# A hybrid S5 and gated DeltaNet trunk on one core: values of the memory by tokens, early inputs of layer 1's output projection, the memory's norm at fixed places

## The chip, the core and the metric

The kernel runs on one core of a Trainium2 chip. A core has five engines with queues of their own, which work in order: TensorE (PE in the profile; it multiplies, and its weight loads are shown as PEld), VectorE (DVE), ScalarE (ACT), GpSimd (POOL) and SyncE (SP, which here only issues DMA transfers). The metric is the device time of one execution in microseconds, lower is better; the median of several runs counts.

## The reference

Two layers run over 1024 tokens of width 1024. Layer 1 has an S5 mixer, layer 2 a gated DeltaNet mixer; each layer also attends to 256 tokens of a memory with 4 heads. Cut to what the change touches:

```python
h = rmsnorm(x, norm_w[i])
mem_h = rmsnorm(mem, mem_norm_w[i])            # 256 x 1024
...                                            # the mixer: y_mix, 1024 x 1536
kv = mem_h @ w_kv[i]                           # 256 x 1024: 512 of keys, 512 of values
y_x = cross_attn(q_x, k, v) * silu(gate_x)     # 1024 x 512
x = x + concatenate([y_mix, y_x]) @ w_out[i]   # 1024 x 2048 by 2048 x 1024
...
return rmsnorm(x, final_norm_w)
```

In the S5 layer, `y_mix` is `y * sigmoid(y @ w_glu + b_glu)` times a gate.

## The kernel before

All large products run in three parts: each operand is split into a rounded high part and a rest (`split`, line 86 the cast by ACT, line 73 the subtraction by DVE), and `mm3` (line 48) issues high x high, high x low, low x high. A weight tile (`weight`) is loaded to `wraw` (512 KB for 128 x 1024), cast to `whi` by ACT, and its rest `wlo` is made by DVE or, with "both", half by DVE and half by POOL. `project` multiplies such tiles with a stack of inputs into PSUM buffers named `pp`, of which there are four; everything small uses four others, `ps_a`.

A scheduler orders each engine's instructions by priority, except where `self.pe.on` keeps TensorE in the order of the code. Tiles come from pools, and a new tile waits until the one that had its memory is done with.

**The head.** `memory_inputs` loads the memory, transposed, as `memT` (4 transfers of 256 KB). `memory(0)` splits it into `mh` and `ml`, weighted by the norm's weights, and then makes eight tiles of `kv`, channels on partitions: each is 24 products over 256 memory tokens. A tile is multiplied by `mrow`, the norm's factor of each token laid along a row, into `kvt`. Tiles 0 to 3 are keys and are stored. Tiles 4 to 7 are values, which the attention wants by tokens: two transposes on TensorE (line 51, `ps_a<-ident,kvt`) and a copy by ACT (`kvu`) follow. The norm itself is `memory_norm`: squares (`msq`), sums (`macc`), the root (`mnv`, `mne`, ...), and two products that spread it (`mndg`).

Beside it run the eight tiles of x: ACT makes `hh`, DVE `hl`, ACT or POOL the square `sq`, DVE adds it to `acc`. Then come two tiles of the S5 input product, `memory(1)` for the second layer, DVE's chain of S5 parameters, and two more tiles.

**The output projection of layer 1.** The twelve gated columns (`w_glu`, inputs `yh` and `yl`) end with a sigmoid and a product on DVE, and each is stored to DRAM as `yT[ct]`. The attention has stored its results as `yT[12]` to `yT[15]`. The 16 inputs of the first half of the tokens are loaded back as `yr` (256 KB each; eight buffers, so eight are loaded ahead) and split into `oh` and `ol`; these tiles lie where tiles of the gate lay, and wait until those are done with. TensorE takes them in the order 12, 13, 14, 15, 0, ..., 11. A second half of the tokens follows.

**The tail.** The last column is done in two blocks of 256 tokens. While the first block is scaled (`out_scale`), DVE works on the norm of the second (`fzv`, `fze`, `fzt`, `fndg`). `beside` names the tiles that ACT and POOL scale instead of DVE.

## Time and profile before

| | |
|---|---|
| median of 3 runs | 1933.11 us (1930.89 to 1936.47) |
| profiled execution, its own time | 1939.14 us |
| its span in the trace | 1937.4 us |
| mean granted clock of TensorE | 0.984 |
| TensorE's first product | 10.98 us after the span's start |
| busy: PE, DVE, ACT, POOL | 96%, 66%, 49%, 5% of the span |

The profiled execution is 6.0 us slower than the median. In rows of the timeline the first two columns are the start, in us from the span's start, and the length; a bracket at the end is the time in which the engine was idle before it, and what ended that. Rows of stretches give the stretch, its length, the engine's busy time with the count of instructions, the granted clock, the DMA engines' share and GB/s.

### The profile page before, as it was taken

The page shows a single profiled execution, that of the slowest core. Times are in us where ns is not written, and L with a number is a line of the kernel's source. Part 1 is how long each engine was busy: PE and PEld are TensorE (multiplying, and loading weights), DVE is VectorE, ACT ScalarE, POOL GpSimd, SP SyncE. Part 2 cuts the span into 40 slices and gives each one's busy share as a digit, 9 for nine tenths or more (in the row PEclk, how much of TensorE's full clock was granted, in tenths as well). Part 3 has the DMA queues.
Part 4 walks back from the last instruction along what each step waited for, and adds up shares of the span by engine and source line. Part 5 has one row for each costly group of instructions (what it writes and reads, how often), then busy time and mean ns, then how long its engine had stood idle before and what let it go on. Part 6 is the DMA issues. An engine that isn't in the chain of part 4 may idle for free.

```text
span 1937.4 us, 28738 instructions
## 1 busy us (share of the span) xinstructions
PE 1865.1 (96%) x10390; PEld 1533.5 (79%) x10390; DVE 1284.0 (66%) x2508; ACT 958.1 (49%) x2043; POOL 95.8 (5%) x65
## 2 busy tenths in 40 slices
PE   6899999999989998999999999999999999899997
PEld 6788888788878887788778878877777888688886
DVE  7988898896565412564455555988743776789744
ACT  5345688786455421543343456665343653544421
POOL 3000000000201221000000000000000000000000
PEclk9999999999999999999999999999999999999999
DMA  7445655655854353654312467676445764876752
GB/s 229 151 136 136 165 170 157 168 155 146 254 167 133 116 173 102 210 164 141 120 56 97 132 199 235 218 224 198 132 117 197 226 202 146 265 231 197 201 161 87
DMA packets 258942, 325.17 MB, mean 168 GB/s; under 512 B 80753, under 2 KB 182705, under 8 KB 258801
## 3 DMA queue, kind: packets, MB, share of 16 engines
q1 hardware_dynamic: 233456, 238.40, 39.9%
q10 hardware_dynamic: 25344, 84.95, 14.7%
q8 instruction: 82, 1.34, 0.3%
q14 instruction: 60, 0.48, 0.1%
HBM read 213.20 MB, written 93.95 MB: 159 GB/s over the span
## 4 chain that ended last, share of the span: by engine, by line
PE 80%; DVE 7%; DMA 6%; ACT 4%; issue 2%; SPq 1%; DVEq 0%; ACTq 0%
PE pp L48 64%; PE ps_a L48 13%; PE ps_a L51 3%; DMA zr<-oTd 1%; SPq L70 1%; DVE wlo L73 1%; DMA yr<-gy 1%; ACT whi L86 0%; DVE pr L77 0%; DMA E<-Grow 0%; DVE ol L73 0%; ACT pr L330 0%; DMA XM<-Dm 0%; DMA R<-E 0%; DMA wraw<-in_s_w_in_dram 0%
## 5 line engine op out<-in xcount | busy, mean ns | idle before, releaser
L48 PE MATMUL pp<-hh,whi 128*128 128x512 f32 x1216 | 496.0, 408 | 0.0
L48 PE MATMUL pp<-hl,whi 128*128 128x512 f32 x1216 | 478.9, 394 | 2.8 <-DVE hl L82 2.8
L48 PE MATMUL pp<-hh,wlo 128*128 128x512 f32 x1216 | 478.0, 393 | 0.0
L86 ACT CAST whi<-wraw 128x1024 fp32r<-128x1024 f32 (+1 forms) x180 | 183.7, 1022 | 370.6 <-PE pp L48 347.0
L73 DVE TENSOR_TENSOR wlo<-wraw,whi 128x1024 fp32r<-128x1024 f32 (+2 forms) x180 | 212.9, 1183 | 94.4 <-ACT whi L86 93.2
L48 PEld LDWEIGHTS pp<-hh,whi 128*128 128x128 f32 x1216 | 229.7, 189 | 50.8 <-issue 5.3
L48 PEld LDWEIGHTS pp<-hh,wlo 128*128 128x128 f32 x1216 | 229.3, 189 | 48.9
L48 PEld LDWEIGHTS pp<-hl,whi 128*128 128x128 f32 x1216 | 230.1, 189 | 46.0 <-DVE hl L82 3.8
L48 PE MATMUL pp<-oh,whi 128*128 128x512 f32 (+1 forms) x528 | 207.8, 394 | 5.7 <-ACT oh L86 5.5
L48 PE MATMUL pp<-oh,wlo 128*128 128x512 f32 (+1 forms) x528 | 210.0, 398 | 0.1
L48 PE MATMUL pp<-ol,whi 128*128 128x512 f32 (+1 forms) x528 | 208.4, 395 | 1.3 <-DVE ol L73 1.3
L48 PEld LDWEIGHTS pp<-oh,whi 128*128 128x128 f32 x528 | 100.9, 191 | 29.0 <-ACT oh L86 7.7
L48 PEld LDWEIGHTS pp<-ol,whi 128*128 128x128 f32 x528 | 100.6, 191 | 25.8 <-DVE ol L73 3.5
L48 PEld LDWEIGHTS pp<-oh,wlo 128*128 128x128 f32 x528 | 101.0, 191 | 21.2 <-DVE wlo L73 0.8
L48 PE MATMUL pp<-yl,whi 128*128 128x512 f32 x288 | 114.2, 396 | 0.4 <-DVE yl L73 0.4
L48 PE MATMUL pp<-yh,wlo 128*128 128x512 f32 x288 | 114.2, 396 | 0.0
L48 PE MATMUL pp<-yh,whi 128*128 128x512 f32 x288 | 113.7, 395 | 0.0
L73 DVE TENSOR_TENSOR pj<-pp,hr 128x512 f32<-128x512 f32 x104 | 69.0, 686 | 54.8 <-PE pp L48 54.8
L73 DVE TENSOR_TENSOR cx<-pp,hr 128x512 f32<-128x512 f32 x48 | 32.5, 689 | 93.6 <-PE pp L48 93.6
L82 DVE SCALAR_TENSOR_TENSOR pj<-cx,conv_w,pj 128x1024 f32<-128x1024 f32 x72 | 92.4, 1283 | 1.4
L48 PEld LDWEIGHTS pp<-yl,whi 128*128 128x128 f32 x288 | 54.4, 189 | 12.4 <-DVE yl L73 0.8
L48 PEld LDWEIGHTS pp<-yh,wlo 128*128 128x128 f32 x288 | 54.4, 189 | 11.9
(363 smaller groups left out, 3109.2 us busy)
## 6 DMA issues: line engine op xcount, KB each, us to landing
wraw<-in_w_out_dram ACTq DMA_DIRECT2D x64, 512.0 KB, 4.1
wraw<-in_g_w_in_dram ACTq DMA_DIRECT2D x44, 512.0 KB, 3.9
wraw<-in_s_w_in_dram ACTq DMA_DIRECT2D x32, 512.0 KB, 4.0
R<-E SPq DMA_DIRECT2D x48, 256.0 KB, 3.9
gate<-pj SPq DMA_DIRECT2D x24, 512.0 KB, 4.4
qkv<-pj SPq DMA_DIRECT2D x24, 512.0 KB, 2.6
kq<-qkv SPq DMA_DIRECT2D x60, 192.0 KB, 4.3
wraw<-in_w_glu_dram ACTq DMA_DIRECT2D x24, 384.0 KB, 3.5
```

What stands on the lines that cost most here:

```text
L48: return self.pin(self.eng.matmul(*a, **kw))
L51: return self.pin(self.eng.transpose(*a, **kw))
L70: self.nc.sync.dma_start(out=out, in_=in_)
L73: (eng or self.v).tensor_tensor(out=out, in0=a, in1=b, op=op)
L82: self.v.scalar_tensor_tensor(out=out, in0=a, scalar=s, in1=b, op0=op0, op1=op1)
L86: self.act.copy(hi, src)
```

## The change

Three parts.

**A. The memory.** The values are computed by tokens: the memory's tokens are now the stationary operand, and two weight tiles side by side the moving one, so the result needs no transpose. There are as many products as before. ACT scales the result with the token's factor, a scalar per partition (`mcol`). The values come first, then the four keys, in the order of the code. The first two joined value weights are loaded among the pieces of `memT`. The two sums of the norm are adds instead of reductions, and its products stand behind the values (`macc`) and behind the third key (`mndg`).

On TensorE, at layer 0's values: before, a value tile's product stood beside the transposes of the tile before.

```order
L48 MATMUL pp<-ml,whi 128x256
L51 MATMUL ps_a<-ident_150,kvt 128x128 x2
L48 MATMUL pp<-mh,wlo 128x256
L51 MATMUL ps_a<-ident_150,kvt 128x128 x2
L48 MATMUL pp<-mh,whi 128x256
```

Now, at the end of the values, where the keys begin:

```order
L48 MATMUL pp<-whi,mh 128x256
L48 MATMUL pp<-wlo,mh 128x256
L48 MATMUL pp<-whi,ml 128x256
L48 MATMUL ps_a<-ones_155,macc_350 128x1 x2
L48 MATMUL pp<-mh,whi 128x256
L48 MATMUL pp<-ml,whi 128x256
```

The first value pair has two buffers of `ps_a`, the second two of `pp`. On ACT, at the first x tiles, it stood before (`kvu` is the copy behind the transposes):

```order
L86 CAST whi<-wraw 128x1024
L278 COPY kvu<-ps_a 128x256 x2
L179 ACTIVATE sq<-x 128x1024
L237 ACTIVATE hh_167<-x,nw_158 128x1024
L86 CAST whi<-wraw 128x1024
L278 COPY kvu<-ps_a 128x256
L86 CAST whi<-wraw 128x1024
```

and now (the cast ahead of the first `hh` waits for the second key's last product that reads the older weight; TensorE's first product of the third key waits for the `kvu<-pp` row):

```order
L86 CAST whi<-wraw 128x1024
L313 ACTIVATE kvu<-ps_a,mcol_381 128x2x128 x2
L86 CAST whi<-wraw 128x1024
L242 ACTIVATE hh_167<-x,nw_158 128x1024
L184 ACTIVATE sq<-x 128x1024
L242 ACTIVATE hh_167<-x,nw_158 128x1024
L184 ACTIVATE sq<-x 128x1024
L313 ACTIVATE kvu<-pp,mcol_381 128x2x128 x2
L242 ACTIVATE hh_167<-x,nw_158 128x1024 x2
```

The scalings moved behind two x tiles.

**B. The projection's inputs.** At gated column 10, five of the 16 inputs of the first half (12 to 15 and 0) are loaded and split into tiles of the attention's pool, which stays open. Ten of the other eleven are loaded straight into `oh` and `ol` tiles that are not yet used and cast in place; the last comes through `yr` (four buffers instead of eight). The stores of `yT[10]` and `yT[11]` are issued by POOL instead of SP. On SP, from the store of column 7 on, before:

```order
L70 DMA yT<-ye 128x1024
L70 DMA ge<-gate_92 128x1024
L70 DMA yT<-ye 128x1024 x3
L70 DMA abw_7022<-in_g_w_ab_dram 128x192
L70 DMA yT<-ye 128x1024
L70 DMA yr<-yT 128x512 x17
```

and now (the two last stores are on POOL):

```order
L70 DMA ge<-gate_92 128x1024
L824 DMA yT<-ye 128x1024 x2
L70 DMA abw_7006<-in_g_w_ab_dram 128x192
L70 DMA oh_7051<-yT 128x512
L70 DMA ol_7055<-yT 128x512
L70 DMA oh_7059<-yT 128x512
L70 DMA ol_7063<-yT 128x512
```

The loads moved ahead of the last stores.

On TensorE, the first row being the last gated product, before:

```order
L48 MATMUL pp<-yh_5230,wlo 128x512
L48 MATMUL pp<-oh_7035,whi 128x512
L48 MATMUL pp<-ol_7036,whi 128x512
L48 MATMUL pp<-oh_7035,wlo 128x512
L48 MATMUL pp<-oh_7037,whi 128x512
```

and now, with the early inputs first:

```order
L48 MATMUL pp<-yh_5190,wlo 128x512
L48 MATMUL pp<-qh,whi 128x512
L48 MATMUL pp<-ql,whi 128x512
L48 MATMUL pp<-qh,wlo 128x512
L48 MATMUL pp<-ph,whi 128x512
L48 MATMUL pp<-pl,whi 128x512
L48 MATMUL pp<-ph,wlo 128x512
L48 MATMUL pp<-ph,whi 128x512
```

Fifteen products on `qh` to `pr` stand where the first `oh` stood; the order of the gated columns and of the attention among them is as before.

**C. The tail.** For the first block of the last column, two more tiles (4 and 6) are scaled by ACT and POOL. On DVE, in the norm's chain of the second block, before:

```order
L77 TENSOR_SCALAR fzh<-fzv 128x2
L82 SCALAR_TENSOR_TENSOR xo_17426<-xo_17426,fnw_159,ps_a 128x256
L79 TENSOR_SCALAR fze<-fze 128x2
L82 SCALAR_TENSOR_TENSOR xo_17562<-xo_17562,fnw_159,ps_a 128x256
L82 SCALAR_TENSOR_TENSOR fzt<-fze,fzh 128x1 x2
```

and now:

```order
L77 TENSOR_SCALAR fzh<-fzv 128x2
L79 TENSOR_SCALAR fze<-fze 128x2
L82 SCALAR_TENSOR_TENSOR fzt<-fze,fzh 128x1 x2
L82 SCALAR_TENSOR_TENSOR fze<-fzt,fze 128x2
L82 SCALAR_TENSOR_TENSOR fzt<-fze,fzh 128x1 x2
```

The two long rows left the chain.

The diff (lines that the memory's old functions lose are left out; they stand above):

```diff
             self.dma(self.mnw, self.A["mnw"])
             self.act.copy(self.once(wp, (128, 1), "table"), self.ones[:, 0:1])
+            self.first = []
+            for q, step in ((0, 2), (1, 4)):
+                w = [self.ring.tile([128, 8, 128], dt, name=n, tag=n)
+                     for n, dt in (("wraw", F32), ("whi", F32R), ("wlo", F32R))]
+                self.first.append(w[1:])
+                for k in range(4 * q, 4 * q + 4, step):
+                    raw, hi, lo = (t.rearrange("p (c k) n -> p c k n", c=2)[:, :, k % 4:k % 4 + step] for t in w)
+                    self.dma(raw, self.A["w_kv"][0, 4:6, :, k:k + step].rearrange("c p k n -> p c k n"))
+                    for j in range(k, k + step, 2):
+                        self.dma(mt[:, j:j + 2], self.A["memT"][j:j + 2].rearrange("k p t -> p k t"))
+                    self.split(raw, hi, lo)
+    def memory_sum(self, wp):
         acc = self.once(wp, (128, 256), "macc")
         for k in range(0, 8, 4):
             sq = self.tl(wp, (128, 4, 256), "msq")
             self.act.activation(sq, self.memT[:, k:k + 4], AF.Square)
             part = acc if k == 0 else self.tl(wp, (128, 256), "kvt", bufs=2)
+            self.tt(sq[:, 0:2], sq[:, 0:2], sq[:, 2:4], ADD)
+            self.tt(part, sq[:, 0], sq[:, 1], ADD)
         self.tt(acc, acc, part, ADD)
+        col = self.negative_rstd(wp, (acc,), 1024, "mn")
+        self.mcol = self.once(wp, (128, 2), "mcol")
+        self.ts(self.mcol, col, -1.0, MUL)
+    def value_weight(self, layer, i, q):
+        ct = 4 + 2 * i
+        return self.weight(self.A["w_kv"][layer, ct:ct + 2, :, 4 * q:4 * q + 4, :].rearrange("c p k n -> p c k n"))
     def memory(self, layer, wp):
         mt = self.memT
         hh, hl = self.tl(wp, (128, 8, 256), "mh", F32R), self.tl(wp, (128, 8, 256), "ml", F32R)
         for k in range(8):
             self.weighted(mt[:, k], self.mnw[:, layer, k:k + 1], hh[:, k], hl[:, k])
+        pairs = []
+        for i in range(2):
+            pool, nm = ((self.pa, "ps_a"), (self.pp, "pp"))[i]
+            ps = [pool.tile([128, 256], F32, name=nm, tag=nm) for _ in range(2)]
+            for q in range(2):
+                w = self.first[q] if layer == i == 0 else self.value_weight(layer, i, q)
+                rows = [t.rearrange("p (c k) n -> p k c n", c=2) for t in w]
+                for j in range(4):
+                    k = 4 * q + j
+                    for b in range(2):
+                        s = slice(128 * b, 128 * b + 128)
+                        self.mm3(ps[b].rearrange("p (c n) -> p c n", c=2), (hh[:, k, s], hl[:, k, s]),
+                                 [t[:, j] for t in rows], k == 0, k == 7)
+            pairs.append(ps)
         if layer == 0:
+            self.memory_sum(wp)
+        def key(ct, ps):
             t = self.tl(wp, (128, 256), "kvt", bufs=2)
             self.tt(t, ps, self.mrow, MUL)
             self.dma(self.kvd[layer][ct], t)
+        def values(i, ps):
+            t = self.tl(wp, (128, 2, 2, 128), "kvu", bufs=1)
+            for b in range(2):
+                self.act.activation(t[:, :, b], ps[b].rearrange("p (c n) -> p c n", c=2), AF.Copy,
+                                    scale=self.mcol[:, b:b + 1])
+            for c in range(2):
+                self.dma(self.kvd[layer][4 + 2 * i + c], t[:, c].rearrange("p b d -> p (b d)"))
+        todo = []
+        for ct in range(4):
+            if ct == (0 if layer else 2):
+                for i, ps in enumerate(pairs):
+                    values(i, ps)
+            ps, = self.project([self.A["w_kv"][layer, ct]], (hh, hl), n=256)
+            todo.append((ct, ps))
+            if layer == 0 and ct == 2:
+                self.mrow = self.once(wp, (128, 256), "mrow")
+                self.rows_to(self.mrow, self.on_partitions(wp, self.mcol, "mn"))
+            if layer or ct >= 2:
+                for one in todo:
+                    key(*one)
+                todo = []
     def scaled(self, out, ps, rb, fn=None):
...
             h = self.hidden(hp)
             with P(name="s5p", bufs=1, side="right") as sp:
                 with P(name="s5tmp", bufs=1, side="right") as tmp, P(name="mem", bufs=1, side="right") as mp:
+                    self.rings = cycle([self.ring, self.ring, mp])
                     self.memory_inputs(mp)
                     self.dma(self.nw, A["nw"])
-                    self.rings = cycle([self.ring, self.ring, mp])
                     with P(name="ld1", bufs=1, side="right") as wp:
                         acc = self.once(wp, (128, L), "acc")
                         xs = []
...
                         self.constants(None)
                         self.wlo_eng, self.wq = "both", self.nc.sync
                         with self.tc.high_priority(offset=self.ahead):
+                            self.pe.on = True
                             self.memory(0, mp)
+                            self.pe.on = False
                         self.wlo_eng, self.wq = self.v, self.nc.scalar
                         for k in range(KD):
                             if k >= 3:
...
                     self.pe.on = True
                     self.s5_groups(wp, steps())
                     self.pe.on = False
-            gs = ExitStack()
+            as1, gs = ExitStack(), ExitStack()
+            ap = as1.enter_context(P(name="at1", bufs=1, side="right"))
             ya = gs.enter_context(P(name="ya", bufs=1, side="right"))
             wp = gs.enter_context(P(name="glu", bufs=2, side="right"))
-            ap = gs.enter_context(P(name="at1", bufs=1, side="right"))
             y = []
             def glu_inputs(n, pool):
...
         for ct in range(12):
             w = A["w_glu"][ct]
             ps = self.project([w[:, 0:6], w[:, 6:12]], y)
+            if ct == 10:
+                early = self.out_inputs(ap, wp)
             e, g = self.tl(wp, (128, L), "ye"), self.tl(wp, (128, L), "ge")
             self.dma(g, self.gate[ct])
             self.tt(e, y[ct][0].bitcast(F32), y[ct][1].bitcast(F32), ADD, self.pool)
...
                 sg = self.tl(wp, (128, 512), "sig")
                 self.act.activation(sg, p, AF.Sigmoid, bias=self.b_glu[:, ct:ct + 1])
                 self.tt(e[:, s], e[:, s], sg, MUL)
-            self.dma(self.yT[ct], e)
+            (self.nc.sync if ct < 10 else self.pool).dma_start(out=self.yT[ct], in_=e)
             for i in range(2):
                 next(attend, None)
         gs.close()
...
             per = lambda t: t.rearrange("p (t k) -> p t k", t=4)
             for half in range(2):
                 hs, ts_ = slice(512 * half, 512 * half + 512), slice(4 * half, 4 * half + 4)
-                y = self.half_tiles(yp, 512, lambda i: 2 if i < 4 else 1)
+                y = self.half_tiles(yp, 512, lambda i: 1, True)
+                if half == 0:
+                    y[:len(early)] = early
                 for i, k in enumerate([12, 13, 14, 15] + list(range(12))):
-                    t = self.tl(xp, (128, 512), "yr", bufs=8)
+                    if half == 0 and i < len(early):
+                        continue
+                    n = i - len(early)
+                    if half == 0 and n < 10:
+                        t = self.tl(yp, (128, 512), f"o{'hl'[n % 2]}{n // 2}")
+                    else:
+                        t = self.tl(xp, (128, 512), "yr", bufs=4)
                     self.dma(t, self.yT[k, :, hs])
                     self.split(t, y[i][0], y[i][1])
                 for ct in range(KD):
...
                     if ct == 0:
                         self.act.activation(av, per(x), AF.Square)
                     else:
-                        sq = self.tl(xp, (128, 512), "sq", bufs=2)
+                        sq = self.tl(ap, (128, 512), "yx")
                         self.act.activation(sq, x, AF.Square)
                         self.tt(av, av, per(sq), ADD)
             col = self.rstd_cols(xp, acc, 1024, "n2")
             self.rows_to(h[2], self.on_partitions(xp, col, "n2"))
+        as1.close()
         return st2, h
-    def half_tiles(self, yp, n, bufs):
-        return [[self.tl(yp, (128, n), f"o{c}{i}", F32R, bufs(i)) for c in "hl"] for i in range(16)]
+    def out_inputs(self, ap, wp):
+        two = [self.tl(ap, (128, 2, 512), nm, F32R) for nm in ("ph", "pl")]
+        tiles = [[self.tl(ap, (128, 512), nm, F32R) for nm in ("qh", "ql")]]
+        tiles += [[t[:, b] for t in two] for b in range(2)]
+        tiles.append([self.tl(ap, (128, 512), nm, F32R) for nm in ("q", "sg")])
+        pr = self.tl(ap, (128, 2, 512), "pr", F32R)
+        tiles.append([pr[:, i] for i in range(2)])
+        for i, y in enumerate(tiles):
+            if i % 2 == 0:
+                raw = self.tl(wp, (128, L), "yr")
+            t = raw[:, 512 * (i % 2):512 * (i % 2) + 512]
+            self.dma(t, self.yT[(12, 13, 14, 15, 0)[i], :, 0:512])
+            self.split(t, *y)
+        return tiles
+    def half_tiles(self, yp, n, bufs, down=False):
+        order = range(15, -1, -1) if down else range(16)
+        y = {i: [self.tl(yp, (128, n), f"o{c}{i}", F32R, bufs(i)) for c in "hl"] for i in order}
+        return [y[i] for i in range(16)]
     def s5_input(self, i, h, wp):
         ps = yield from self.project_by_k([self.A["s5_w_in"][i]], h)
...
         with self.tc.high_priority(offset=200):
             col = self.negative_rstd(wp, (acc[:, blocks[1]], sq), 1024, "fz")
             last = self.on_partitions(wp, col, "fn", -1.0)[0]
-        self.out_scale(wp, xo, rb, 1, blocks[0], (1, 3, 5, 7))
+        self.out_scale(wp, xo, rb, 1, blocks[0], (1, 3, 4, 5, 6, 7))
         self.out_scale(wp, xo, last, 1, blocks[1])
     def out_scale(self, wp, xo, rb, half, s, beside=(2, 5)):
```

22 lines of the change are left out of this document (5 added, 17 removed).

## The prediction

> **What bounds the kernel now.** I read the page first (busy time and the chain that ended last), then the waits of TensorE, then the granted clock stage by stage, then the single instructions around the places that the change touches.
>
> ```profile
> PE 1865.1 (96%) x10390; PEld 1533.5 (79%) x10390; DVE 1284.0 (66%) x2508; ACT 958.1 (49%) x2043; POOL 95.8 (5%) x65
> PE 80%; DVE 7%; DMA 6%; ACT 4%; issue 2%; SPq 1%; DVEq 0%; ACTq 0%
> ```
>
> TensorE is busy for 96% of the span and carries 80% of the chain (shares of the span by engine). So a change that leaves the products alone can win two things only: the 72 us in which TensorE is idle (span 1937.4 less 1865.1), and time in which it is busy at a lower clock. These are its waits (columns: us in all, times, longest) at the three places that the change touches:
>
> ```profile
> PE pp L48 <- ACT whi L86: 11.0, 1, 11.0
> PE pp L48 <- ACT oh L86: 5.5, 2, 3.6
> PE ps_a L51 <- DVE kvt L73: 5.2, 2, 2.8
> PE ps_a L48 <- DVE fndg L79: 4.0, 1, 4.0
> ```
>
> 11.0 is the start of the program, 5.2 the transposes of the values, 5.5 the start of layer 1's output projection, 4.0 the last norm. Two of these carry a second price, shown by the granted clock (the figure behind TensorE's count, here in some stretches):
>
> ```profile
> 40.70:44.10 3.40, 3.40 (x18) 0.50 0.93 298
> 44.10:47.40 3.30, 3.30 (x29) 1.00 0.76 274
> 95.30:98.70 3.40, 3.40 (x19) 0.50 0.57 196
> 771.10:781.40 10.30, 8.21 (x18) 0.50 0.71 242
> ```
>
> Behind each such wait a stretch runs at half clock: 18 products in 3.4 us where 29 fit at full clock, so some 1.7 us are lost in each 3.4. At 771.1 the stretch is three times as long, because a second wait falls into it, and of its 8.21 busy us half, 4.1, is lost.
>
> **Part A, the head.** Before, TensorE's start is set by the order of loads: memory first, then the first weight.
>
> ```profile
> 4.91 1.71 ACT L237 ACTIVATE mh<-memT,mnw 128x256 fp32r<-128x256 f32 x4 [2.62 <-DMA memT<-in_memT_dram]
> 9.88 1.05 ACT L86 CAST whi<-wraw 128x1024 fp32r<-128x1024 f32 x1 [0.40 <-DMA wraw<-in_w_kv_dram]
> 10.98 0.58 PE L48 MATMUL pp<-mh,whi 128*128 128x256 f32 x1 [10.98 <-ACT whi L86]
> 12.44 1.98 ACT L86 CAST whi<-wraw 128x1024 fp32r<-128x1024 f32 x2
> 23.23 0.41 PE L48 MATMUL pp<-ml,whi 128*128 128x256 f32 x1
> 23.44 0.36 PE L48 MATMUL pp<-mh,wlo 128*128 128x256 f32 x1
> 23.76 0.28 PE L48 MATMUL pp<-ml,whi 128*128 128x256 f32 x1
> 14.32 1.15 ACT L237 ACTIVATE hh<-x,nw 128x1024 fp32r<-128x1024 f32 x1
> 28.75 1.06 ACT L179 ACTIVATE sq<-x 128x1024 f32<-128x1024 f32 x1
> 39.52 0.44 PE L51 MATMUL ps_a<-ident,kvt 128*128 128x128 f32 x2 [2.81 <-DVE kvt L73]
> 65.48 1.88 PE L48 MATMUL ps_a<-ones,acc 128*128 128x1 f32 x16
> ```
>
> The memory's first 256 KB have landed when the first mh starts, at 4.9. Afterwards these first 256 KB are half of a joined weight, and the memory's come second. The cast of half a weight is 0.5 (half of 1.05), one mh 0.43 (1.71/4), so TensorE starts at about 6 instead of 10.98. Then it runs short again. The other half of the joined weight stands 1.5 MB deep in the queue, as the first weight did before: there at 9.9, cast by 10.9, four more mh by ACT to 12.6, and on DVE the lower half (1.2) and four ml (as long as the mh) to 13.8. I put the end of the first value pass at 14.5. The second pass takes the next two weights; before, the second and third were there at 12.44, but now ACT has first to do those mh and the second square of the memory, so their casts run from 13.7 on, and their lower halves follow to 18.7. At the cold pitch of 0.21 (23.23 to 23.44), which in the trace lasts 12.5 us from the first product, I put the end of the second pass at 22.5. That is 96 products. Before, the 96th is near 30: the 48th near 24, since the clock rises at 23.6, and 48 more at 0.12 (3.3/29, a little more with the row of the norm) end there. The lead is 7.5 us. Two key tiles of 24 products at 0.12 and the sum of squares follow, to 28.7.
>
> Then comes a wait that before doesn't have. The two pairs of value sums hold their PSUM buffers until ACT has scaled them, and the third key tile needs the buffer of pp that the second pair holds. Its scaling is the row kvu<-pp in ACT's order. Ahead of it in the same queue stand a cast that itself waits for the end of the second key tile (28.7), and two each of hh and sq: 1.05 + 2 x 1.15 + 2 x 1.06 = 5.5 us. So TensorE stands from 28.7 to about 34.9, and a half-clock stretch follows (1.7). The last key tile ends at 28.7 + 6.2 + 48 x 0.12 + 1.7 = 42.4, against 47.4 before: 5 us of lead.
>
> From there to 77 the x tiles bound both kernels, on DVE:
>
> ```profile
> 45.00:70.00 25.00, 22.19 (x115) 18.10 (x114) 23.01 (x33) 12.42 (x19) 4.59 (x2) 1.00 0.42 145
> 70.00:105.00 35.00, 32.56 (x238) 30.80 (x237) 31.08 (x123) 13.28 (x23) 0.00 (x0) 0.95 0.54 162
> 44.77 1.27 DVE L82 SCALAR_TENSOR_TENSOR hl<-x,nw,hh 128x1024 fp32r<-128x1024 f32 x1
> 41.71 2.81 DVE L73 TENSOR_TENSOR acc<-acc,sq 128x1024 f32<-128x1024 f32 x1 [0.78 <-ACT sq L179]
> 47.77 1.22 DVE L73 TENSOR_TENSOR acc<-acc,sq 128x1024 f32<-128x1024 f32 x1
> 91.92 0.42 DVE L73 TENSOR_TENSOR kvt<-pp,mrow 128x256 f32<-128x256 f32 x1 [2.07 <-DMA kv<-kvt]
> 126.37 1.37 DVE L73 TENSOR_TENSOR pj<-pp,hr 128x512 f32<-128x512 f32 x2 [0.42 <-PE pp L48]
> ```
>
> DVE is busy for 23.01 of 25 us there. Afterwards seven hl (1.27) and seven acc (three of 2.8, beside POOL's sq, and four of 1.22), three weight halves (1.22) and four kvt follow the new wait's first hh at about 31: 8.9 + 13.3 + 3.7 + 1.7 = 27.6, so the norm's sum is at 58.5 instead of 65.5. Lead 7. Layer 1's memory tiles then lose the second transposes' wait (2.4) and its half clock (1.7): lead 11 on TensorE. DVE gains less: 7, four kvt (1.7) and the 2.07 idle at 91.92, at most 10.8; it is busy for 31.08 of 35 us there. I take 9. Behind 105 nothing of the change stands in TensorE's order until 767, so the lead is kept. Ends: 3, when the new wait costs twice what I give it, and 12.
>
> The removed transposes themselves, the kvu copies (now scalings by ACT, as many) and the two reductions (now adds) stand beside this and are in the figures.
>
> **Part B, the projection's start.**
>
> ```profile
> 770.74 0.50 PE L48 MATMUL pp<-oh,whi 128*128 128x512 f32 x1 [3.63 <-ACT oh L86]
> 775.83 0.80 PE L48 MATMUL pp<-oh,whi 128*128 128x512 f32 x1 [1.86 <-ACT oh L86]
> 769.82 0.35 ACT L86 CAST abw<-abw 128x192 fp32r<-128x192 f32 x1 [1.13 <-DVE wlo L73]
> 775.16 4.83 ACT L86 CAST oh<-yr 128x512 fp32r<-128x512 f32 x9 [3.95 <-issue]
> 775.81 6.18 DVE L73 TENSOR_TENSOR ol<-yr,oh 128x512 fp32r<-128x512 f32 x10 [3.79 <-ACT oh L86]
> 770.02 0.32 SPq L70 DMA_DIRECT2D yT<-ye  x1
> 771.44 12.25 SPq L70 DMA_DIRECT2D yr<-yT  x13
> DMA to landing us min/median/max: 2.8/5.7/6.6
> ```
>
> TensorE loses 3.63 + 1.86 idle and 4.1 by the clock: 9.6. [...]
>
> The second wait is a store's: the nine casts of 775.16 start when the store issued at 770.02 has landed, 5.1 later, since one of their tiles lies where the stored column lay.
>
> Afterwards 15 products on the five early tiles run on from 767.1 (770.74 less 3.63) at 0.21: 3.2 us, to 770.3. The first late tile is cast after the abw cast of 769.82, from 770.1: 0.6 + 0.65 for its lower half, ready at 771.3. Then DVE makes one in 0.62 (6.18/10), TensorE eats one in 0.64 (three products); one weight's cast and lower half lie between (1.23). That leaves 1.0 + 1.2 = 2.2 us of idle in pieces of about 1; I charge no clock for them, since the shortest wait seen here with a half clock behind it is above 1.8. Gain 9.6 - 2.2 = 7.4, ends 5 (the clock falls once and 0.7 more is idle) and 9.6. For the raw loads I name the cover: they are issued from about 755 on, as soon as the last gated column has read the y tiles that lay there, and 15 us hide them. Their cover is gone if SP stops at one of them: each later one would then cost its 0.94 (12.25/13).
>
> The last tile, yT[11], cannot be early. Its store now stands on POOL's queue, and no row here shows a DMA that POOL issues. Bounds from SP's rows: 2.8 to 6.6 for the store, the same for the load. From 770.0: 770.0 + 2 x 2.8 + 1.25 = 776.9, or 770.0 + 13.2 + 1.25 = 784.5. It is needed as the 16th, at 767.1 + 15 x 0.64 + 2.2 = 778.9. With the queue emptied of thirteen loads I stand near the lower end: nothing, range 0 to 5.6, or 8 with a half-clock stretch. [...]
>
> **Part C, the tail.**
>
> ```profile
> 1924.26 2.77 POOL L73 TENSOR_TENSOR xo<-xo,fr 128x256 f32<-128x256 f32 x4 [61.89 <-ACT fr L1379]
> 1926.35 0.47 DVE L82 SCALAR_TENSOR_TENSOR xo<-xo,fnw,ps_a 128x256 f32<-128x256 f32 x1
> 1926.97 0.47 DVE L82 SCALAR_TENSOR_TENSOR xo<-xo,fnw,ps_a 128x256 f32<-128x256 f32 x1
> 1929.43 1.22 PE L48 MATMUL ps_a<-fndg,ones 128*128 128x128 f32 x4 [4.05 <-DVE fndg L79]
> ```
>
> Two scalings (0.47 each) leave DVE's short chain from the last sum to fndg, 0.94 less the gaps that they filled: 0.75. POOL takes two more at 0.69 and ends at 1928.4, ahead of its next use. Ends: 0 and 0.95.
>
> **The sum.** 9 + 7.4 + 0.75 = 17.2. The profiled execution took 1939.1 us, 6.0 above the median of the runs shown. 1939.1 - 17.2 = 1921.9 in its terms, and 1933.1 - 17.2 = 1915.9 for the median. A difference under 0.3% (5.8 us) can hardly be told from none.
>
> **The rivals.**
> 1. The head pays the new wait twice (a late x tile, or a half clock that lasts) or DVE passes on nothing: 3 of 9. Sum 11.2, time 1922. For it: DVE's 23.01 of 25. Against it: DVE has less to do. Chance 0.2.
> 2. The late tile costs B its clock: 7.4 - 5.6 - 1.7, nearly nothing. Sum 9.8, time 1923. For it: 6.6 us landings in this very place. Against it: the loads that crowded it have gone. Chance 0.12.
> 3. The leads meet other waits: the head's lead ends at DVE's parameter chain, which at 126.37 is only 0.42 ahead of TensorE, and B keeps only the 3.2 us of early products. Sum 4.0 (3.2 and 0.75), time 1929. Chance 0.07.
> 4. Slower, by one mechanism: the third key tile waits for ACT's in-order queue, and behind it waits every hh. Each us by which the second key tile ends later than 28.7 is a us of that chain. At 28.7 + 9 = 37.7 the head has gained nothing; at 45.9 the whole change has; beyond it, it loses, 1945 at 58. It would need value weights 17 us later than the loads before have been. Chance 0.04.
> 5. [...] Chance 0.05. [...]
> 6. The first case, 13 to 22 of gain: 0.52; its own range 1911 to 1920.
>
> Together faster 0.88 (1, 2, 5 and 6 but for a hundredth), same 0.07, slower 0.05. The range reaches to rivals 1 and 2 and to both upper ends (12 + 9.6 + 0.95 = 22.6, time 1910.5), with 2 us for the run: 1909 to 1926.
>
> **What would show it.** A: the first product near 6; no transposes of kvt; a new row in which pp waits for kvu, of 4 to 7 us; the norm's sum near 58.5; layer 1's last memory tile near 95 instead of 104.9. B: after the last gated column 15 products without a break, no wait above 1.5, clock 1.00 from 771 to 781. C: fndg's wait 3.3 instead of 4.0. Wrong would be: a wait at the third key tile over 12 us, a wait for yT[11] above 2, half clock at 775, or a new wait between 105 and 750, where the order of the products is unchanged.

## The result and the profile after

| | before | after |
|---|---|---|
| median of 5 runs each, beside each other | 1933.11 us (1930.22 to 1936.47) | 1920.21 us (1918.05 to 1924.84) |
| profiled execution, its own time | 1939.14 us | 1918.05 us |
| its span, mean granted clock | 1937.4 us, 0.984 | 1916.3 us, 0.989 |

The ratio after to before is 0.9942, 95% interval 0.9927 to 0.9957: 11.2 us of gain, between 8.3 and 14.1, where 17.2 was forecast. The whole time, 1920.2, is inside the range, above the likeliest case's own 1911 to 1920 by a hair.

The first lines of the page after (busy time, and the chain that ended last):

```profile
PE 1853.1 (97%) x10374; PEld 1524.4 (80%) x10374; DVE 1284.2 (67%) x2501; ACT 957.5 (50%) x2046; POOL 98.6 (5%) x67
PE 76%; DVE 8%; DMA 8%; ACT 4%; issue 2%; SPq 1%; POOL 0%; DVEq 0%; ACTq 0%; POOLq 0%
```

TensorE is busy 12.0 us less than in the profile of before and idle 63.2 us instead of 72.3. Its waits after, at the places of the change:

```profile
PE ps_a L48 <- ACT mh L242: 6.3, 3, 5.4
PE pp L48 <- ACT kvu L313: 5.8, 1, 5.8
PE ps_a L48 <- DVE fndg L79: 4.8, 1, 4.8
PE pp L48 <- DVE wlo L73: 2.2, 1, 2.2
PE pp L48 <- DVE hl L82: 1.7, 1, 1.7
```

The start costs 5.4 instead of 11.0. The new wait of the third key tile is there, 5.8. The projection's waits for `oh` (5.5) are gone from the list. The tail's wait for `fndg` has grown from 4.0 to 4.8.

The two profiled spans differ by 21.1 us, the medians by 12.9. Part of the rest lies at waits that both kernels have. Stretches of the profile of before (columns as in the prediction: length, busy time of PE, PEld, DVE, ACT, POOL, then the granted clock):

```profile
354.70:361.50 6.80, 6.11 (x21) 4.58 (x22) 5.14 (x8) 3.57 (x7) 0.00 (x0) 0.50 0.32 71
566.30:573.10 6.80, 5.49 (x16) 4.49 (x17) 3.99 (x6) 1.91 (x3) 1.10 (x1) 0.50 0.20 78
962.30:969.10 6.80, 6.80 (x22) 4.20 (x22) 3.09 (x16) 0.00 (x0) 0.74 (x1) 0.50 0.00 1
```

and of the profile after, around the same work:

```profile
350.00:358.00 8.00, 6.36 (x43) 5.46 (x44) 7.83 (x13) 5.61 (x9) 0.00 (x0) 1.00 0.60 174
560.00:568.00 8.00, 7.95 (x37) 6.28 (x38) 3.56 (x7) 3.60 (x5) 0.00 (x0) 1.00 0.55 160
940.00:970.00 30.00, 27.35 (x139) 19.56 (x137) 15.41 (x40) 14.33 (x25) 0.74 (x1) 1.00 0.10 29
```

Half of the 18.4 busy us in the first three rows, 9.2, is lost there by the clock, and none after. The waits at these places are nearly alike: the longest one ahead of the first stretch is 1.86 in both profiles, and 1.86 again in a second profile of the changed kernel, which has half clock behind it; at the second stretch both have one of 1.92, and before has another of 1.61. So those 9.2 us can't be put down to the change: a single pair of profiles can't be subtracted as a whole, and the stages are compared one by one below.

### The profile page after: what moved, and what is told of

Same layout as the page of the kernel before. It is cut to its first block, busy times and chain, and to the rows that moved or that the text cites. A ratio compares the mean times of both kernels' runs of the same rounds, so it can differ in the third digit from the quotient of the medians.

```text
span 1916.3 us, 28676 instructions
## 1 busy us (share of the span) xinstructions
PE 1853.1 (97%) x10374; PEld 1524.4 (80%) x10374; DVE 1284.2 (67%) x2501; ACT 957.5 (50%) x2046; POOL 98.6 (5%) x67
## 4 chain that ended last, share of the span: by engine, by line
PE 76%; DVE 8%; DMA 8%; ACT 4%; issue 2%; SPq 1%; POOL 0%; DVEq 0%; ACTq 0%; POOLq 0%
PE pp L48 60%; PE ps_a L48 13%; PE ps_a L51 3%; DMA yr<-gy 1%; SPq L70 1%; DVE wlo L73 1%; DMA kq<-qkv 1%; ACT whi L86 1%; DMA E<-Grow 1%; ACT pr L382 0%; DVE E L73 0%; DVE XN L73 0%; DMA XM<-Dm 0%; DMA vT<-qkv 0%; DMA zr<-yT 0%
## 5 line engine op out<-in xcount | busy, mean ns | idle before, releaser
L86 ACT CAST whi<-wraw 128x1024 fp32r<-128x1024 f32 (+2 forms) x181 | 183.6, 1015 | 362.6 <-PE pp L48 332.0
L48 PE MATMUL pp<-ol,whi 128*128 128x512 f32 (+1 forms) x488 | 191.1, 392 | 1.4 <-DVE ol L73 1.4
L48 PE MATMUL pp<-oh,whi 128*128 128x512 f32 (+1 forms) x488 | 191.3, 393 | 0.3
L48 PE MATMUL pp<-oh,wlo 128*128 128x512 f32 (+1 forms) x488 | 191.5, 393 | 0.0
L48 PEld LDWEIGHTS pp<-ol,whi 128*128 128x128 f32 x488 | 92.2, 189 | 23.3 <-DVE ol L73 3.6
L48 PEld LDWEIGHTS pp<-oh,whi 128*128 128x128 f32 x488 | 92.4, 189 | 21.4 <-ACT oh L86 1.9
L48 PEld LDWEIGHTS pp<-oh,wlo 128*128 128x128 f32 x488 | 92.4, 189 | 19.1 <-DVE wlo L73 0.3
L48 PEld LDWEIGHTS pp<-yl,whi 128*128 128x128 f32 x288 | 54.1, 188 | 12.5 <-DVE yl L73 1.1
L48 PEld LDWEIGHTS pp<-yh,whi 128*128 128x128 f32 x288 | 54.1, 188 | 11.8 <-ACT yh L86 0.2
```

The costliest lines, as they stand in the source:

```text
L48: return self.pin(self.eng.matmul(*a, **kw))
L86: self.act.copy(hi, src)
```

## The experiments

Every kernel was profiled once; those with a ratio were also timed in several rounds beside the kernel before. The milestones (us from the span's start) are the starts of single products in the timeline of TensorE: the norm's sum over x (`ps_a<-ones,acc`), the first and the last product of layer 1's memory tiles, and, as a length, from the last product of the last gated column (`yh`) to the last product of the sum of layer 2's norm.

| kernel | median us, ratio (interval) | norm's sum | layer 1's memory tiles | gated column to layer 2's sum | wait for fndg |
|---|---|---|---|---|---|
| before | 1933.1 | 65.5 | 77.1 to 104.6 | 196.5 | 4.05 |
| after (A, B, C) | 1920.2, 0.9942 (0.9927-0.9957) | 59.7 | 78.8 to 101.5 | 187.8 | 4.76 |
| the same again | 1921.3, 0.9939 (0.9917-0.9962) | 61.0 | 76.7 to 99.4 | 188.4 | 4.76 |
| without A | 1923.7, 0.9953 (0.9933-0.9972) | 62.2 | 75.3 to 101.2 | 187.6 | 4.76 |
| without B | 1925.0, 0.9957 (0.9942-0.9973) | 59.2 | 75.0 to 97.7 | 195.2 | 4.76 |
| without C | 1916.2, 0.9921 (0.9904-0.9937) | 59.3 | 78.3 to 101.0 | 191.2 | 4.05 |
| A in layer 1 alone | 1921.6, 0.9955 (0.9938-0.9971) | 63.7 | 75.2 to 97.9 | 188.6 | 4.76 |
| values scaled first | 1915.0, 0.9912 (0.9895-0.9928) | 62.2 | 73.3 to 97.6 | 188.2 | 4.75 |
| values first, no C | 1916.5, 0.9924 (0.9901-0.9946) | 60.7 | 75.6 to 100.0 | 188.0 | 4.05 |
| values first, no C, store by ACT | 1919.7, 0.9936 (0.9913-0.9959) | 61.7 | 75.6 to 99.3 | 189.7 | 4.05 |
| last store before loads | 1924.8, 0.9954 (0.9934-0.9973) | 60.5 | 76.3 to 98.9 | 194.1 | 4.76 |
| no loads in place | 1921.8, 0.9947 (0.9930-0.9963) | 58.4 | 74.3 to 97.0 | 192.5 | 4.76 |

The intervals are some 6 us wide, wider than most single terms; the stages of the traces resolve more than the times do.

### One part undone at a time

**Without A** (the memory's functions and loads as before, TensorE not kept in the code's order there):

```diff
-                            self.pe.on = True
                             self.memory(0, mp)
-                            self.pe.on = False
```

> Parts B and C alone; the memory is as before. By theory 1 (the traces: the projection's start gave 8.7 us, the head 3, the tail nothing or a small loss) about 8 us are left, 1925, 0.996 of before; first product near 11.0, the projection's start as in the changed kernel, without half clock there. By theory 2 (the prediction's head of 9 us is real and one trace hid it, so of the 11 to 13 us only 3 or 4 are the projection's) 1929 to 1930, 0.998.

**Without B** (stores of all twelve columns by SP, all 16 inputs through eight `yr`, no early tiles):

```diff
-            if ct == 10:
-                early = self.out_inputs(ap, wp)
-            (self.nc.sync if ct < 10 else self.pool).dma_start(out=self.yT[ct], in_=e)
+            self.dma(self.yT[ct], e)
```

> Parts A and C alone; the projection's inputs are as before. By theory 1 (head 3, tail minus 0.7) 1930 to 1931, 0.999 of before, with the two waits for oh and the half clock behind them back at the projection's start. By theory 2 (head 9) 1924, 0.995.

**Without C:**

```diff
-        self.out_scale(wp, xo, rb, 1, blocks[0], (1, 3, 4, 5, 6, 7))
+        self.out_scale(wp, xo, rb, 1, blocks[0], (1, 3, 5, 7))
```

> Parts A and B alone; two tiles are back on DVE in the tail. By theory 1 the short steps of DVE's norm were stretched while POOL worked beside them (fzt 1.32 instead of 0.34), so the wait for fndg falls from 4.8 back to 4.0 and the kernel is 0.7 us faster than the changed one, 1919.5. By theory 2 (the prediction: two steps of 0.47 left the chain) the wait is longer than in the changed kernel, and the kernel 0.75 us slower. The times can hardly tell 0.7 us; the wait for fndg in the trace does.

**The changed kernel again**, for the spread between two sets of runs:

> The changed kernel itself, as the measure for the three others on this chip. By theory 1 and theory 2 alike 0.992 to 0.995 of before. Theory 1 adds: wait for fndg 4.76 us, wait at the third key tile 5.5 to 7.5, and no wait above 1.5 at the late inputs of the projection; by theory 2 fndg's 4.76 was one trace's chance and lies near 3.3 to 4.1 here.

Measured: rows of the table. By the ratios, undoing A gives back 2.4 us (0.9953 less the 0.99405 that is the mean of the two runs of the changed kernel, times 1931), undoing B 3.2, and undoing C gains 3.8. These differences are within the intervals, and they don't add up: they give the three parts 2.4 + 3.2 - 3.8 = 1.8 us, where all three together are worth 11.2 and 11.8. What the rest is, some 10 us, is not settled; with intervals of 3 us to each side on every kernel the three differences together are uncertain by about as much (an estimate). Much of the scatter lies where no edit was made: from layer 1's last memory product to the last gated column, and from layer 2's sum to the products on `fndg`, the profiles of the other kernels take 1614.2 to 1626.8 us together, before 1630.4. The lowest is the kernel without C, so only 0.7 of its 3.8 us can be put down to C.

The texts set down ahead of these runs fare unevenly by the times. Without A, 0.9953 is nearest to the first theory's 0.996. Without B, 0.9957 is the second theory's figure (0.995, a head worth 9 us) and its interval leaves out the first theory's 0.999; the stages below contradict that head. The changed kernel again has its 6.7 us at the third key tile and 4.76 for `fndg`, as the first theory had it.

The stages say more. Without B TensorE waits at the projection as it did before (timeline of TensorE, without B):

```profile
758.51 0.80 PE L48 MATMUL pp<-oh,whi 128*128 128x512 f32 x1 [3.62 <-ACT oh L86]
763.63 0.80 PE L48 MATMUL pp<-oh,whi 128*128 128x512 f32 x1 [1.89 <-ACT oh L86]
```

These are nearly the 3.63 and 1.86 of before, and the stage takes 195.2 us. With B as changed, nine profiles give 187.6 to 191.2, mean 188.5; without it the two give 195.9. B is worth 7.4.

For A, layer 1's last memory product starts at 102.9 in the mean of the two kernels without it, and at 99.3 in the mean of the eight that have it unaltered (after, again, without B, without C, two of part B, two of the tail below): 3.6. That figure is loose: the two lie at 104.6 and 101.2, so it is 5.3 against the one and 1.9 against the other, and the eight spread from 97.0 to 101.5. Where it comes from is the next group.

### Where A's lead is made, and lost

Without A, and after, the stretch of layer 1's memory tiles. Without A:

```profile
75.30:101.25 25.95, 23.65 (x199) 23.36 (x198) 23.79 (x87) 11.78 (x22) 0.00 (x0) 1.00 0.65 198
0.00:101.70 101.70, 80.25 (x536) 72.49 (x537) 86.80 (x211) 50.37 (x73) 21.22 (x18) 0.98 0.60 193
```

After:

```profile
78.80:101.50 22.70, 22.70 (x193) 22.70 (x192) 22.53 (x90) 13.72 (x31) 0.00 (x0) 1.00 0.62 185
0.00:102.00 102.00, 84.43 (x522) 77.33 (x523) 85.34 (x225) 52.88 (x85) 17.08 (x16) 0.92 0.57 187
46.00:78.80 32.80, 30.17 (x132) 24.45 (x131) 26.89 (x79) 9.36 (x16) 2.87 (x1) 0.90 0.29 92
```

and before, from the start to the same place:

```profile
0.00:105.00 105.00, 84.01 (x536) 77.38 (x537) 86.29 (x211) 50.78 (x73) 19.68 (x18) 0.97 0.58 187
```

In layer 1 TensorE is busy all of 22.7 us after, with no break. Over the whole head it is idle for less (length less busy): 17.6 us in the mean of the eight profiles with A unaltered, 21.2 in the mean of before and without A. These 3.6 us are the 3.6 of the milestones. But it is not busy for less: 82.1 us in both means, though 16 transposes of 0.27 us are gone.

Part of what they gave is lost to the clock. It stands at 0.92 after instead of 0.97 or 0.98; time lost by it is about one less the clock times the stretch: 8.2 us after, 3.2 before, 2.0 without A. With A unaltered the eight profiles lose 4.9 to 8.2, mean 6.9; that is 4.3 more than the mean of before and without A. This count leaves out the start of the program, where the column says 1.00 though products come at half the pace: from 18 to 21 us TensorE starts 15 of them before, and 28 without A, whose memory is the same. So before's pace rises late (at 23.6, as the prediction read it; near 17 without A, near 9 after), which makes up an estimated 3 us of its 104.6, half of 23.6 less 17. How much of the transposes' time the clock took back can't be told to the microsecond.

**A in layer 1 alone.** Layer 0's memory, its loads and the norm as before the change, only layer 1's values by tokens:

```diff
-                            self.pe.on = True
-                            self.memory(0, mp)
-                            self.pe.on = False
+                            self.memory_old(0, mp)
```

> Layer 0's memory is as before the change (memory first, then the weights; channel-major values with their transposes; reductions in the norm), and only layer 1's values are made token-major; the projection's early inputs and the tail stay changed. Theory 1: the head's gain lies in layer 1's memory tiles alone, which last 22.7 us token-major against 26 to 27.5 with transposes. So here the first product starts near 11, there is no wait of the third key tile, layer 1's tiles last 22.7 us and end at 98 to 100 (99.2 is the mean with the whole part, 102.9 without), and the time is within 2 us of the changed kernel's, at a ratio of .993 to .995. Theory 2: the early start in layer 0 carries the gain: the tiles end near 103 and the time is that of the kernel without the memory part, 3 to 4 us above the changed kernel's.

```profile
75.20:97.90 22.70, 22.70 (x192) 22.66 (x192) 22.64 (x89) 13.16 (x28) 0.00 (x0) 1.00 0.73 219
0.00:98.40 98.40, 79.35 (x530) 72.15 (x531) 86.43 (x215) 51.86 (x80) 19.25 (x18) 0.98 0.62 199
```

The layer-1 tiles start at 75.2, as they do without A (75.3), last 22.7 as after, and end at 97.9, 3.3 earlier than without A and earlier than in six of the eight kernels with the whole part. The trace bears out the first theory: what A gains by this point, it gains in layer 1, and the reordered layer 0 with its earlier start adds nothing that shows. In the mean of the eight, layer 0's memory ends at 44.7 and layer 1's tiles start at 76.6; in the three kernels with the old layer 0 (before, without A, this one) it is 44.7 and 75.9. The time (0.9955) is 0.0005 above the ratio that the theory gave, and by the medians within 2 us of the changed kernel's (2.8 us by the ratios); it can't tell the theories apart.

**Values scaled first.** The second value pair of layer 0 is scaled by ACT into two free `kvt` tiles (they needn't wait for the first pair's store), and both scalings get a high priority, so they stand ahead of the x tiles:

```diff
+            if layer == 0 and i == 1:
+                two = [self.tl(wp, (128, 256), "kvt", bufs=2) for _ in range(2)]
+                for b in range(2):
+                    for c in range(2):
+                        self.act.activation(two[c][:, 128 * b:128 * b + 128], ps[b][:, 128 * c:128 * c + 128],
+                                            AF.Copy, scale=self.mcol[:, b:b + 1])
...
-                for i, ps in enumerate(pairs):
-                    values(i, ps)
+                with self.tc.high_priority(offset=2000):
+                    for i, ps in enumerate(pairs):
+                        values(i, ps)
```

> All three parts, but for layer 0 the second pair of values is scaled into the two kvt buffers, so that it needs not wait for the first pair's store, and both scalings stand ahead of the x tiles on ACT. By theory 1a the wait of 5.8 us at the third key tile goes to under 1.5, but DVE's work on the x tiles bounds the stage, so the norm's sum comes at most 2 us earlier than 59.7 and the kernel gains 0 to 3 us over the changed one, 1917 to 1920, 0.992 to 0.994 of before. By theory 1b (TensorE's wait and its half clock are the stage's limit) 6 to 9 us, 1912 to 1914, 0.990.

Its waits of TensorE in the head, and the stretch from layer 0's last memory product to layer 1's first:

```profile
PE ps_a L48 <- DVE n1dg L77: 4.1, 3, 3.5
PE pp L48 <- DVE hl L82: 2.0, 2, 1.5
```

```profile
37.30:73.30 36.00, 27.91 (x127) 21.15 (x126) 34.19 (x65) 15.74 (x21) 7.71 (x3) 0.99 0.48 159
```

The wait of the third key tile is gone and layer 0's memory ends at 37.3 instead of 46.0. Of these 8.7 us 5.5 are left at layer 1's first tile (73.3 against 78.8), 3.8 at the end of these tiles, and only 1.7 against the mean of the eight (99.3): DVE is busy for 34.19 of 36.0 us and makes TensorE wait for `n1dg` instead. That is the other bound of the head. The norm's sum comes at 62.2, later than after's 59.7, where the first theory had it up to 2 us earlier, and layer 1's tiles take 24.3 us at a clock of 0.95. The ratio, 0.9912, lies between the two theories' figures.

**Values first, without C**, alone and with the last column's store on ACT's queue:

```diff
-            (self.nc.sync if ct < 10 else self.pool).dma_start(out=self.yT[ct], in_=e)
+            (self.nc.sync if ct < 10 else self.pool if ct == 10 else self.act).dma_start(out=self.yT[ct], in_=e)
```

> The values scaled first as in e4, part C undone, and the store of yT[11] on ACT's queue instead of POOL's. By theory 1 the three add up: 4 us at the memory (e4's trace), 0.7 at the tail, and up to 1 where the last late input came just in time; 5 to 6 us faster than e5, 0.989 to 0.990 of before. By the rival (the chance of the clock is all that e4 won) 0 to 2 us faster than e5.

> Both value pairs of layer 0 are scaled before the x tiles (as in the run that scaled them first), and the tail scales as before the change. Theory 1: the two differences add. Then TensorE does not wait at the third key tile, layer 0's memory ends near 37.5 instead of 46, the wait for fndg is 4.05 instead of 4.76, and the time is 4 to 8 us below the changed kernel's, at a ratio near .990. Theory 2: only the 0.7 us at the tail is real, since DVE's x tiles bound the head whatever TensorE does there, and the better medians of the two single edits came by chance. Then layer 1's memory tiles still start at 73 to 76 and end at 97 to 100, and the ratio is .992 to .9945.

Layer 1's tiles end at 99.3 and 100.0, and the ratios are 0.9936 and 0.9924. With the store on ACT's queue the projection's stage takes 189.7, within the 187.6 to 191.2 of the others; that kernel is 1.6 us faster than the changed kernel again, as its rival had it (0 to 2). The second theory of the last text fits: no sum of the two single edits shows, and of their better medians only the tail's 0.7 us is sure.

### What carries B

**Last store before the loads.** The store of `yT[11]` goes back to SP, where the scheduler puts it ahead of the late loads:

```diff
-            (self.nc.sync if ct < 10 else self.pool).dma_start(out=self.yT[ct], in_=e)
+            (self.nc.sync if ct != 10 else self.pool).dma_start(out=self.yT[ct], in_=e)
```

> The store of yT[11] is back on SP's queue, ahead of the eleven late loads (that of yT[10] stays on POOL's). By theory 1 the loads then wait for the last gated column as in before: TensorE is idle for about 3 to 4 us behind the 15 early products, with a half clock behind it, and 4 to 6 us of part B's 8.7 are lost, 1924 to 1926. By the rival (POOL's queue is the slow one, the loads are hidden either way) within 1 us of e5, and the last late input comes sooner.

```profile
766.09 0.80 PE L48 MATMUL pp<-oh,whi 128*128 128x512 f32 x1 [5.85 <-ACT oh L86]
```

The loads wait behind the store on SP, TensorE stands for 5.85 us at the first late input, and the stage takes 194.1: 5.6 of B's 7.4 are gone, though the five early tiles are still there. The time, 1924.8, is in the first theory's range.

**No loads in place.** All late inputs come through the four `yr`:

```diff
-                    if half == 0 and n < 10:
-                        t = self.tl(yp, (128, 512), f"o{'hl'[n % 2]}{n // 2}")
-                    else:
-                        t = self.tl(xp, (128, 512), "yr", bufs=4)
+                    t = self.tl(xp, (128, 512), "yr", bufs=4)
```

> The five early inputs stay, but the eleven late ones come through the four yr buffers instead of straight into oh and ol. By theory 1 (the late loads must be under way before the last column ends) the first four are loaded early, the other seven wait for a buffer and take 2.4 us and more each round: idle 3 to 6 us behind the ninth input and half clock, 1924 to 1928. By the rival (the early inputs alone carry part B) 0 to 1.5 us slower than e5.

```profile
766.12 0.62 PE L48 MATMUL pp<-oh,whi 128*128 128x512 f32 x1 [1.74 <-ACT oh L86]
775.27 0.50 PE L48 MATMUL pp<-oh,whi 128*128 128x512 f32 x1 [1.71 <-ACT oh L86]
```

Two waits, 3.5 us in all, and a stage of 192.5: by this one profile the loads in place carry some 4 us of B's 7.4. The median, 1921.8, doesn't show it: it is 0.5 us above the changed kernel again, as the rival had it. So the store on a queue of its own and the late loads in place are both needed for B's whole gain in the stage. The early inputs were not taken out alone; what they are worth without the other two is at most the 1.8 us that were left with the store back on SP.

### The tail

C undone (above) gave 4.05 for the wait. To see why C makes it longer, the tiles that ACT and POOL scale were varied; `out_scale`'s list is `()`, then `(1, 3)`:

```diff
-        self.out_scale(wp, xo, rb, 1, blocks[0], (1, 3, 4, 5, 6, 7))
+        self.out_scale(wp, xo, rb, 1, blocks[0], ())
```

> For the first block of the last column DVE makes all eight scalings, and ACT and POOL none. If POOL's products stretch DVE's short steps, the first two fzt steps take about 0.17 each (1.32 for two with six POOL products, 0.34 with four that end earlier), but up to eight scalings of 0.47 may stand in DVE's chain, so the wait for fndg is about 0.47 for each scaling that the order puts ahead of it. If instead the fzt steps are slow for another reason, they stay at 1.3 for two.

> Only tiles 1 and 3 are scaled by ACT and POOL; DVE makes six. If POOL's products stretch DVE's short steps, two of them (about 1.4 us) end before the fzt steps begin, which then take 0.34 for two, and the wait for fndg is 4.0 us plus up to 0.9 for two more scalings of 0.47 in the chain. If the stretch has another cause, the pair stays at 1.3.

POOL and DVE in the timeline after:

```profile
1902.31 4.13 POOL L73 TENSOR_TENSOR xo<-xo,fr 128x256 f32<-128x256 f32 x6 [61.89 <-ACT fr L1465]
1903.93 0.49 DVE L77 TENSOR_SCALAR fze<-fzv 128x2 int32<-128x2 int32 x1
1904.45 0.65 DVE L79 TENSOR_SCALAR fze<-fze 128x2 int32<-128x2 int32 x1
1905.13 1.32 DVE L82 SCALAR_TENSOR_TENSOR fzt<-fze,fzh 128x1 f32<-128x1 f32 x2
1906.68 0.35 DVE L82 SCALAR_TENSOR_TENSOR fzt<-fze,fzh 128x1 f32<-128x1 f32 x2
```

with no product on POOL:

```profile
1901.56 0.16 DVE L79 TENSOR_SCALAR fze<-fze 128x2 int32<-128x2 int32 x1
1902.01 0.34 DVE L82 SCALAR_TENSOR_TENSOR fzt<-fze,fzh 128x1 f32<-128x1 f32 x2
1905.15 1.23 PE L48 MATMUL ps_a<-fndg,ones 128*128 128x128 f32 x4 [4.63 <-DVE fndg L79]
```

and with two:

```profile
1901.13 1.41 POOL L73 TENSOR_TENSOR xo<-xo,fr 128x256 f32<-128x256 f32 x2 [61.89 <-ACT fr L1465]
1903.74 0.34 DVE L82 SCALAR_TENSOR_TENSOR fzt<-fze,fzh 128x1 f32<-128x1 f32 x2
1906.35 1.22 PE L48 MATMUL ps_a<-fndg,ones 128*128 128x128 f32 x4 [4.10 <-DVE fndg L79]
```

The same two `fzt` steps take 1.32 us while POOL's six products run (1902.31 to 1906.44), 0.35 just after them, and 0.34 where POOL has none or has finished. Each `fzt` step beside a POOL product lasts about 0.66, one such product (4.13 / 6 = 0.69). Laid end to end at that length (an estimate), the products end at 1904.38, 1905.06 and 1906.44, and the three stretched rows end just behind them, at 1904.42, 1905.10 and 1906.45. The stretch is POOL's doing. The wait by tiles beside DVE: none 4.63, two 4.10, four 4.05, six 4.76. (The single times, 1915.0 and 1916.3, are one run each and say nothing of a difference of 0.7.) Not every step of DVE is stretched beside POOL: the scaling `xo<-xo,fnw,ps_a` keeps its 0.47 (at 1903.54 after, at 1926.35 and 1926.97 before), and `fzh` its 0.15 (at 1904.33 after). What makes the difference no run shows.

## Why the prediction was right and wrong

**A: the gain of 9 was 3.6; the failed step is the lead that was carried from DVE to TensorE.** The head's timeline after (TensorE, and ACT's queue at the new wait):

```profile
5.42 0.58 PE L48 MATMUL ps_a<-whi,mh 128*128 128x256 f32 x1 [5.42 <-ACT mh L242]
17.83 0.36 PE L48 MATMUL pp<-wlo,mh 128*128 128x256 f32 x1 [2.17 <-DVE wlo L73]
37.19 0.58 PE L48 MATMUL pp<-mh,whi 128*128 128x256 f32 x1 [5.83 <-ACT kvu L313]
59.70 3.08 PE L48 MATMUL ps_a<-ones,acc 128*128 128x1 f32 x16 [0.49 <-DVE acc L73]
78.79 0.28 PE L48 MATMUL ps_a<-whi,mh 128*128 128x256 f32 x1
```

```profile
31.27 1.04 ACT L86 CAST whi<-wraw 128x1024 fp32r<-128x1024 f32 x1 [0.30 <-PE pp L48]
36.66 0.84 ACT L313 ACTIVATE kvu<-pp,mcol 128x256 f32<-128x256 f32 x2 [0.36 <-DMA kv<-kvu]
```

- The first product came at 5.42, where 6 was forecast. The wait of the third key tile has the mechanism and nearly the size that was given, 5.83 against 6.2: the scaling stands behind the cast that waits for the second key tile and two x tiles. It also waited 0.36 for the store of the first pair, since `kvu` has one buffer; that was overlooked.
- It came later, though. The wait of 2.17 for a lower half, inside the second value pass, was not in the working, nor was the half clock from 19.2 to 22.7 behind it, and the second key tile ended at 31.4 instead of 28.7, although the slow pace of the start, put down with 12.5 us, ended after about 4.
- The clock was priced at 1.7 behind the new wait. The profile after has 6.8 us of half clock from 36.3, which is 3.4, and the head as a whole lost 4.3 us more to the clock than in the mean of before and without A (the start left out), where the working let it lose 1.7 and win back 1.7 at each of the transposes' waits. So layer 0's memory ended at 46 instead of 42.4, and the 5 us of lead that TensorE was given there were nothing (43.0 without A; 44.7 in both means above).
- The norm's sum came at 59.7, where 58.5 was forecast: of DVE's lead of 7, 5.8 were there in this pair (4.4 in the means, 59.3 against 63.8 with the old layer 0). But it doesn't decide when layer 1's memory tiles start. They stand on TensorE behind the products of the S5 input, and TensorE is busy nearly all the way from layer 0's last memory product: 27.19 of 30.0 us before (first row below), and after 30.17 of 32.8, of which about 3.3 are the clock of 0.90. The interval from the norm's sum to these tiles grew from 11.6 to 19.1, and all of the lead was spent there.
- The gain in layer 1 itself (2.4 idle and 1.7 of clock) is real: 22.7 us instead of 27.5 before (second row), or 26.0 without A, where the clock cost nothing.

```profile
47.10:77.10 30.00, 27.19 (x134) 21.61 (x133) 27.59 (x66) 12.87 (x20) 4.59 (x2) 1.00 0.36 121
77.10:104.60 27.50, 25.06 (x199) 24.84 (x198) 23.99 (x87) 12.19 (x22) 0.00 (x0) 0.94 0.63 187
```

The sum by measured terms is 3.6 + 7.4 - 0.7 = 10.3, against 11.2 (8.3 to 14.1) by the ratio; with the 1.9 and 5.3 for A it would be 8.6 to 12.0. It is near the first rival's 11.2, by that rival's second clause (DVE passes on nothing) and by a part of the first: the new wait was not twice as long, but the half clock behind it was.

**B: 7.4 forecast, 7.4 measured.** The mechanism was right; that the figures are equal is luck. After the last gated column the products run without a break. Three waits of 0.2 for `ol` are left, where 2.2 us in pieces were charged, since products of the next column on the early inputs stand between the late ones (at 766.96 and 770.93); and the clock holds:

```profile
757.90:768.00 10.10, 9.76 (x41) 7.16 (x39) 8.41 (x12) 7.50 (x13) 0.54 (x1) 1.00 0.64 214
768.00:778.00 10.00, 9.55 (x40) 7.04 (x39) 5.76 (x8) 5.98 (x9) 0.00 (x0) 1.00 0.84 301
```

This pair of profiles differs by 8.7 in the stage; the mean, 7.4, holds the kernel without C, which had a late input. The late tile, `yT[11]`, came just in time:

```profile
761.69 0.54 POOL L824 DMA_DIRECT2D yT<-ye  x1 [16.04 <-DVE ye L73]
```

```profile
770.41 0.62 ACT L86 CAST oh<-yr 128x512 fp32r<-128x512 f32 x1 [0.42 <-DMA yr<-yT]
```

Its store landed 4.0 us after POOL issued it (the one before it, 4.7), the load in 4.3 us: 8.3 together, where the lower bound counted 5.6. ACT had waited 0.42 us for it, and TensorE didn't wait. In the kernel without C an earlier one of the late inputs came 1.43 too late, a half clock followed, and that stage took 191.2: there is no margin.

For the idle pieces of about 1 us the prediction charged no clock, since the shortest wait that it had seen with a half clock behind it was above 1.8. A shorter one has it too: behind that wait of 1.43 the products from 769.14 to 771.87 took 0.63 to 0.80, as at half clock before (0.63 at 772.06), where those just ahead of the wait took 0.39 or 0.40. Behind the wait of 2.17 that ended at 17.83 after, the clock from 19.2 to 22.7 was 0.51. But it isn't sure to fall either: behind the second 1.71 of the kernel without loads in place, the products from 775.27 to 777.26 took 0.39 to 0.50. In the traces of before and after all 17 half-clock stretches outside the program's end last 3.4 us (11 of them), 6.8 (5) or 10.2 (one). What decides whether a short wait has one behind it no run shows.

**C: a gain of 0.75 was forecast, it is a loss of 0.7.** The step that failed is that POOL's two more products cost nothing since they end before POOL's next use. The two scalings did leave DVE's chain (0.94), but beside POOL's longer work the second `fze` step grew from 0.31 to 0.65 and the two `fzt` steps from 0.34 to 1.32. The cost of POOL's work lies on DVE. The profile of before had the sign of it already: the same form of step took 0.17 without POOL and 0.49 beside its four products.

```profile
1920.12 0.17 DVE L77 TENSOR_SCALAR fne<-fnv 128x2 int32<-128x2 int32 x1
1925.88 0.49 DVE L77 TENSOR_SCALAR fze<-fzv 128x2 int32<-128x2 int32 x1
1926.74 0.31 DVE L79 TENSOR_SCALAR fze<-fze 128x2 int32<-128x2 int32 x1
1927.36 0.34 DVE L82 SCALAR_TENSOR_TENSOR fzt<-fze,fzh 128x1 f32<-128x1 f32 x2
```

**Whole.** No rival from the slow side came; none of the waits that would have shown the prediction wrong appeared. But two of its signs failed: layer 1's last memory tile at 101.5 instead of 95, and `fndg`'s wait at 4.76 instead of 3.3. That the time is faster was right for two of three reasons; the size was 6 us too large, because the head was counted on the wrong engine (5.4) and the tail had the wrong sign (1.4).

## What to carry to other kernels

A lead counts only on the engine that the next stage really waits for (here 5.8 us of DVE's lead at the norm's sum, and none of it at layer 1's memory tiles): find what stands ahead of that stage in each engine's queue, not just when its last input is ready. Removing a wait early in a stage bound by two engines buys only the distance to the second one (with the values scaled first, of 8.7 us at the end of layer 0's memory 5.5 were left at layer 1's first tile); what was removed inside a run of products that nothing else bounds (layer 1's transposes) was still there at the end of that run, 22.7 us against 26.0. Work moved to POOL had a price on DVE, whose steps are the critical ones in this tail: beside POOL's products an `fzt` step took 0.66 us instead of 0.17 and the second `fze` step 0.65 instead of 0.16, while a scaling kept its 0.47.

No version here clearly beats the changed kernel: the three with the lowest medians (without C, values scaled first, values first without C; 1915.0 to 1916.5) overlap it in their intervals. Undoing C is the one edit whose gain, 0.7 us at the wait for `fndg`, shows in each of its three traces.
